# Another order of seven- and eight-product steps, other planned durations, and held-back first loads in a planner-ordered attention trunk

## The chip, the cores and the metric

The kernel runs on one core of one Trainium2 chip. The metric is the time of one execution on the device, in microseconds. Five engines of the core matter here: TensorE (PE in the profile) multiplies matrices, VectorE (DVE) and ScalarE (ACT) work on elements, GpSimd (POOL) and SyncE (SP) issue transfers.

## The reference

One layer of a decoder: RMS norm of x, projection to q, k, v and a gate, attention in which every weight is a product of sigmoids (stick breaking), a SiLU gate, an output projection, the residual, and a last RMS norm. All is float32.

```python
D_MODEL, SEQ, N_HEADS, HEAD_DIM = 4096, 256, 32, 128

def attn_branch(xn, w_in, w_out):              # w_in (4096, 16384), w_out (4096, 4096)
    q, k, v, g = jnp.split(xn @ w_in, 4, axis=-1)
    o = stick_breaking_attention(to_heads(q), to_heads(k), to_heads(v))
    return (o * jax.nn.silu(g)) @ w_out

def one_block(qb, k, v):                        # of 128 queries, for every head
    z = qb @ k.T / sqrt(128)
    log_fail = where(causal, log_sigmoid(-z), 0)
    suffix = reverse_cumsum(log_fail) - log_fail
    a = where(causal, exp(log_sigmoid(z) + suffix), 0)
    return a @ v

h = x + attn_branch(rms_norm(x, norm_attn), w_in, w_out)
return rms_norm(h, final_norm)
```

## The kernel before

**Numbers.** TensorE works on float32 numbers cut in two: a high part (a cast by ScalarE, `wh` for weights) and a low part (the number minus its high part, by VectorE, `wl`). Every product of two blocks is three matmuls of 128x128 by 128x512: high by high, high by low, low by high (`mm3`, L792). The left operands are the stationary forms, `sh` and `sl` for x, `oh` and `ol` for the heads' outputs.

**Units and steps.** The columns of the weights are worked on in 20 units, one after the other: units 0 to 15 are w_in (two heads each: 256 columns of q, k, gate and v), units 16 to 19 are w_out (1024 columns each). A unit has 16 steps, one for each 256 rows of the weights. In a step, two tiles of weights of 512 KB each are loaded (`raw`, by SyncE in two transfers each) and multiplied as a 2x2 matrix of blocks with the 2x2 matrix of the left side. There are three ways to do it. Units 0 and 16 are plain: eight products into four accumulators. In all other units a step has eight products (`EIGHT_PARTS`, L82) or, in the manner of Strassen and Winograd, seven (`SEVEN_PARTS`, L76), into accumulators b1 to b7, each one bank of PSUM, which are combined only once, at the end of a unit. The list `SEVEN` (L43) says which ten of the sixteen steps have seven. In the last unit (19), the steps run in the order `LAST_STEPS` (L50) and those in `EIGHT_LAST` (L52) have eight.

A seven takes one product less, but more of the other engines. Its weights are four parts: one whole tile, half a tile, and two whole tiles of sums and differences. VectorE computes three whole lows (`wl`, 128x1024), a half low (it lies in a tile of the `wh` kind, so the profile calls it wh<-raw,wh) and three sums (raw<-raw,raw twice and raw<-raw, `sums`, L406). A fourth sum is made by GpSimd with a transfer that adds in place (`add_block`, L383). An eight takes two whole lows and no sum. Five places exist for whole lows (`LOWS`), seven for highs and seven for raw tiles.

**The end of a unit.** `combine` (L688) empties the accumulators into two tiles, `qk_sb` and `gv_sb`. Its order on VectorE is: add bank 6 to gv_sb, add bank 7 to gv_sb, scale and add bank 2 to qk_sb, then bank 4 to qk_sb, then bank 5 to both halves of gv_sb, then bank 3. Bank 4 waits for `early`, which is banks 6 and 7 on VectorE and three scalings on ScalarE. A bank can be written by the next unit only when it is empty. The next unit's step 0 is an eight, and takes banks 2, 2, 4, 4, 5, 5, 3, 3.

**Heads.** In the steps after a unit of w_in, the attention of its two heads runs between the products (`head`, L809; `gate`, L775): transposes, scores, a scan and the output on TensorE, some element-wise work on ScalarE and VectorE. The heads' results go to DRAM and come back as the left side of w_out.

**Who sets the order.** All instructions are emitted in an order found by a planner, `Plan` (L105), that simulates five engines while the program is built. Pieces of work ask for an engine with a cost, from `vector_ns`, `scalar_ns` and `tensor_ns` (L93 to L102), and a key; whenever an engine is free, the planner gives it the ready piece with the lowest key (`turn`, L221). A piece that depends on another is ready only when the simulated engine has finished that one; meanwhile the engine takes another that is ready. What comes out is a fixed order for each engine; on the chip the engines then run those orders with semaphores for the dependencies, at the durations that the chip has. Nothing of the planner runs on the chip.

A key is a time at which the result is due, counted in products: `PRODUCT` = 3 x `tensor_ns(512)` (L302) is 680.25 ns, `first[n]` is when part n of the weights is first used, `place_of[u, s]` when step s of unit u begins. Lows have `first[n]`, or 4 us earlier for the first two parts of a seven (L440); casts 2 us earlier still; sums 3 us before their use (L416). The evictions of `combine` have the start of the next unit, `place_of[u + 1, 0]`, plus 0 to 4 ns (L691), on ScalarE 2 us less. `ten` (L335) is the heads' work on TensorE; it has precedence over products.

**The first loads.** `load` (L364) issues the raw tiles in the order of their use, each as soon as one of the seven places for raw tiles is free. In unit 0 the left side is loaded and cut at the same time: `blocks_of` (L535) loads 256 KB of x transposed (`xs`) for each step through the same queue of SyncE, once the step four before has been used, and writes the stationary forms `sh` and `sl` that step needs; at its end it tells ("form", "s", step). Blocks of x for the norm (`xr`) go through that queue too.

Of the kernel before, what the change touches and what calls it, by code (L numbers as in the profile page):

```python
# [28 lines left out]
W = 2 * CW  # L29
# [10 lines left out]

SEVEN = (1,3,4,6,7,9,10,12,13,14)  # L43
RAW_BUFS = 7
HIGHS = 7
LOWS = 5
ROWS = 4
SINGLES = 2

LAST_STEPS = (0, 1, 2, 3, 5, 4, 6, 13, 7, 8, 9, 14, 10, 12, 11, 15)  # L50

EIGHT_LAST = (12, 13, 14)  # L52
KEPT = 5
LAST_ORDER = (5, 4, 2, 3)

# [4 lines left out]
ON_SCALAR = ((1, 3, 5), (1, 3))  # L60
AHEAD, SUMS_AHEAD = 4.0, 3.0
BLOCKS_LATER = 2


PLAIN = {"C11": 1, "C21": 6, "C12": 7, "C22": 3}
# [33 lines left out]


def tensor_ns(n):
    return 0.4167 * n + 13.4 if n > 128 else 109.0  # L102


class Plan:  # L105
# [135 lines left out]
def kernel(  # L241
# [41 lines left out]
    for u, (kind, w, cols) in enumerate(units):  # L283
        for s in (step_at(u, k) for k in range(NS)):
            quads.append(tuple((w, c, s) for c in cols))
            if kind == "plain":
                which = [plain_part(0, PLAIN["C11"], PLAIN["C21"]), plain_part(1, PLAIN["C12"], PLAIN["C22"])]
            else:
                which = SEVEN_PARTS if s in SEVEN and not (u == LAST and s in EIGHT_LAST) else EIGHT_PARTS
            for i, (k, place, prods) in enumerate(which):  # L290
                parts.append(
                    dict(u=u, s=s, i=i, tile=(len(quads) - 1, k), place=place, prods=prods, quad=len(quads) - 1,
                         seven=which is SEVEN_PARTS, size=place.stop - place.start)
                )
# [24 lines left out]
        return nc.here + 1e3 * c  # L319


    def dve(emit, n, key=None, **kw):
        n = n if isinstance(n, tuple) else (n,)
        cost = sum(vector_ns(m) for m in n) + 122 * (len(n) - 1)
        return nc.work("vector", cost, emit, soon() if key is None else key, **kw)

    def act(emit, n, key=None, **kw):
# [5 lines left out]
    FULL_P, FULL_S = (P,) * 2, (W,) * 2  # L333

    def ten(emit, *n):  # L335
        return nc.work("tensor", 90 + sum(tensor_ns(m) for m in n), emit, nc.here - 1e4, wait=400)

    def moved(engine, emit, sizes, key, after=None, hold=False, adds=False, wait=0):
        issue = 550 if engine == "gpsimd" else 330
# [24 lines left out]
    def load():  # L364

        seven = [parts[quad_parts[q][0]]["seven"] for q in range(len(quads))]
        tiles = [(2 * q - 1.5 if t and seven[q] else 2 * q + t, q, t) for q in range(len(quads)) for t in range(2)]
        for _, q, t in sorted(tiles):
            w, blocks, s = quads[q][t]
            yield nc.take("raw")  # L370
            r = raw[q, t] = wp.tile([P, HG, KT, CW], F32, tag="raw", name=f"raw{q}_{t}", bufs=RAW_BUFS)
            if t and seven[q]:
                nc.start(add_block(q))

            def both():
# [30 lines left out]
    def sums(q):  # L406

        a, b, c, d = quad_parts[q]
        one, two = raw[q, 0], raw[q, 1]
        for k in range(2):  # L410
            tile_left[q, k] += 1

        def add(to, at_, f, g, key, op=ALU.add):
            return dve(
                lambda: nc.vector.tensor_tensor(out=to[:, :, at_, :], in0=f, in1=g, op=op), W,
                key - SUMS_AHEAD * 1e3,  # L416
            )

        yield nc.until(("lows", a), ("T3", q))
        yield add(one, 0, one[:, :, 0, :], two[:, :, 0, :], first[c], ALU.subtract)  # L420
        yield nc.until(("lows", b))
        yield add(two, 1, one[:, :, 0, :], two[:, :, 1, :], first[c])
        nc.tell(("sums", c))
        yield add(one, 1, one[:, :, 0, :], one[:, :, 1, :], first[d])
        nc.tell(("sums", d))
        for k in range(2):
            tile_done(q, k)
# [5 lines left out]
    def piece(n, c, there):  # L433

        p = parts[n]
        yield nc.until(*there)
        full = raw[p["tile"]][:, :, p["place"], :][:, :, c, :].rearrange("p i c (h e) -> p c i h e", e=RUN)
        h = wh[n][:, c]
        size = (c.stop - c.start) * W
        key = first[n] - (AHEAD * 1e3 if p["seven"] and p["i"] < 2 else 0)  # L440
        yield act(lambda: nc.scalar.copy(h, full), size, key - 2.0 * 1e3)
        if p["size"] == KT:
            if c.start == 0:
                yield nc.take("wl")
                wl[n] = by_runs(wp.tile([P, KT * W], F32R, tag="wl", name=f"wl{n}", bufs=LOWS))
                nc.tell(("lowslot", n))
            else:
                yield nc.until(("lowslot", n))
        l = wl[n][:, c]
        if n == 0:  # L450
            yield nc.until(("sh", c.start))
        yield dve(lambda: minus(l, full, h), size, key)
        for k in range(c.start, c.stop):
            nc.tell(("low", n, k))
        low_done(n)
# [33 lines left out]
    forms = {}  # L489

    def new_forms(i, what):
        n = len(SEVEN_FORMS if i in SEVEN else EIGHT_FORMS)
        h = sp.tile([P, n, P], F32R, tag=f"xh{i}", name=f"{what}h{i}")
        l = sp.tile([P, n, P], F32R, tag=f"xl{i}", name=f"{what}l{i}")
        forms[i] = h, l
        return h, l
# [18 lines left out]
    def sums_of(i, y, what, key):  # L515

        tt = nc.vector.tensor_tensor
        if i not in SEVEN:
            yield from differences(i, y, key)
        else:  # L520

            def four():
                tt(out=y[:, 0, :], in0=y[:, 1, :], in1=y[:, 0, :], op=ALU.subtract)
                tt(out=y[:, 1, :], in0=y[:, 3, :], in1=y[:, 1, :], op=ALU.subtract)
                tt(out=y[:, 3, :], in0=y[:, 0, :], in1=y[:, 3, :], op=ALU.subtract)
                tt(out=y[:, 2, :], in0=y[:, 2, :], in1=y[:, 3, :], op=ALU.add)

            yield dve(four, (P, P, P, P), key)
            yield from both_parts(i, slice(4, 7), y[:, 1:4, :], key)

# [157 lines left out]
    def combine(u, one, two, what):  # L688

        bank = ev[u]  # L690
        key = place_of[u + 1, 0]  # L691

        row = [rs["v"][:, t : t + 1] if u < OUT0 else 1.0 for t in range(NT)]

# [3 lines left out]
        def add_scaled(to, b, f, n, t):  # L698
            if u >= OUT0:
                return add(to, b, f, n)  # L700
            return dve(
                lambda: nc.vector.scalar_tensor_tensor(
                    out=to, in0=bank[b], scalar=row[t], in1=f, op0=ALU.mult, op1=ALU.add
                ),
                W, key + n,
            )

        def scaled(to, f, t):
# [231 lines left out]
    def blocks_of_heads(s):  # L940
# [9 lines left out]
        yield from both_parts(s, slice(0, 4), y, key)  # L950
        nc.tell(("form", "o", s))
        key = min(place_at(OUT0, s + SUMS_LATER), place_of[OUT0 + 1, s] - 3e3)
        if s in SEVEN and s < NS - 1:
            nc.give("gh")
            yield nc.until(("used", OUT0, s))
            y = yield from heads_of(s, key)
# [358 lines left out]
```

## Time and profile before

| what | value |
|---|---|
| time, median of 3 runs | 1736.43 us (1734.35 to 1738.91) |
| the profiled execution | 1736.38 us, of which the profile's span is 1734.4 us |
| mean granted clock of TensorE | 0.998 of full speed |
| ScalarE, GpSimd: busy share | 70%, 19% |
| first product of unit 0, of unit 1, of unit 16 | 5.9 us, 96.5 us, 1386.2 us |
| last matmul | 1722.5 us |

How to read it: the profile is of one execution. PE, DVE, ACT, POOL and SP are the engines; a busy share is the time in which an engine executes, so what is left is waiting. Nearly all instructions are issued through one helper, so they all carry the line L124, and one goes by the names of the tiles, written out<-in: acc<-wh,sl is a matmul of a weight's high part with a low left side into an accumulator. A wait names whose result ended it. In a timeline, a row has the start, the duration, the engine, the operation and the tiles, and a number in brackets is the time that the engine was idle before it; consecutive instructions of one kind are one row with a count. Engines overlap the end of one instruction with the start of the next, so durations add up to more than the distance of the starts.

### The profile page before, as it was taken

The page shows a single profiled execution, that of the slowest core. Times are in us where ns is not written, and L with a number is a line of the kernel's source. Part 1 is how long each engine was busy: PE and PEld are TensorE (multiplying, and loading weights), DVE is VectorE, ACT ScalarE, POOL GpSimd, SP SyncE. Part 2 cuts the span into 40 slices and gives each one's busy share as a digit, 9 for nine tenths or more (in the row PEclk, how much of TensorE's full clock was granted, in tenths as well). Part 3 has the DMA queues.
Part 4 walks back from the last instruction along what each step waited for, and adds up shares of the span by engine and source line. Part 5 has one row for each costly group of instructions (what it writes and reads, how often), then busy time and mean ns, then how long its engine had stood idle before and what let it go on. Part 6 is the DMA issues. An engine that isn't in the chain of part 4 may idle for free. (4 is left out here: it accounts for less than half of the span.)

```text
span 1734.4 us, 25312 instructions
## 1 busy us (share of the span) xinstructions
PE 1709.5 (99%) x7735; PEld 1413.1 (81%) x7735; DVE 1634.4 (94%) x2106; ACT 1209.9 (70%) x1640; POOL 334.7 (19%) x407
## 2 busy tenths in 40 slices
PE   9999999999999999999999999999999999999997
PEld 7788788888888888888888888888888888888785
DVE  8889999999999999999999999999999987999997
ACT  8976767676767676767676767676767675666654
POOL 0012222222222222222212222222222112112220
PEclk9999999999999999999999999999999999999999
DMA  9968887879787878787879787979787978899895
GB/s 361 313 170 237 224 237 219 242 215 249 206 256 207 256 207 256 209 258 203 262 199 263 200 258 201 258 197 260 198 257 198 284 237 249 244 269 259 229 305 190
DMA packets 249385, 413.82 MB, mean 239 GB/s; under 512 B 28129, under 2 KB 73441, under 8 KB 249249
## 3 DMA queue, kind: packets, MB, share of 16 engines
q1 hardware_dynamic: 194544, 354.24, 61.6%
q0 software_dynamic: 54416, 57.70, 20.4%
q8 instruction: 60, 0.98, 0.2%
q14 instruction: 77, 0.62, 0.1%
q10 hardware_dynamic: 288, 0.28, 0.0%
HBM read 403.98 MB, written 8.13 MB: 238 GB/s over the span
## 5 line engine op out<-in xcount | busy, mean ns | idle before, releaser
L124 ACT CAST wh<-raw 128x1024 fp32r<-128x1024 f32 (+1 forms) x995 | 922.3, 970 | 379.6 <-DVE raw L124 183.0
L124 DVE TENSOR_TENSOR wl<-raw,wh 128x1024 fp32r<-128x1024 f32 (+1 forms) x818 | 974.6, 1217 | 67.5 <-PE acc L124 31.3
L124 PE MATMUL acc<-wh,sh 128*128 128x512 f32 x2048 | 784.8, 395 | 8.1 <-DVE qk_sb L124 7.6
L124 PE MATMUL acc<-wh,sl 128*128 128x512 f32 x1898 | 732.8, 386 | 0.5 <-DVE sl L124 0.5
L124 PE MATMUL acc<-wl,sh 128*128 128x512 f32 x1748 | 675.7, 387 | 1.5 <-DVE wl L124 1.5
L124 POOL DMA_DIRECT2D raw<-in_w_in_dram x300 | 262.2, 982 | 1046.1 <-DMA raw<-in_w_in_dram 423.5
L124 PEld LDWEIGHTS acc<-wh,sh 128*128 128x128 f32 x2048 | 384.6, 188 | 92.4 <-DVE qk_sb L124 13.6
L124 PEld LDWEIGHTS acc<-wh,sl 128*128 128x128 f32 x1898 | 355.8, 187 | 73.8 <-DVE sl L124 1.0
L124 PEld LDWEIGHTS acc<-wl,sh 128*128 128x128 f32 x1748 | 328.3, 188 | 63.9 <-DVE wl L124 4.4
L124 DVE TENSOR_TENSOR raw<-raw,raw 128x512 f32<-128x512 f32 x354 | 242.3, 684 | 6.8 <-DMA raw<-in_w_in_dram 2.8
L124 PE MATMUL acc<-wh,oh 128*128 128x512 f32 x512 | 194.3, 388 | 0.0
L124 PE MATMUL acc<-wh,ol 128*128 128x512 f32 x485 | 187.1, 386 | 0.0
L124 PE MATMUL acc<-wl,oh 128*128 128x512 f32 x458 | 177.3, 387 | 1.9 <-DVE wl L124 1.9
L124 DVE TENSOR_TENSOR wh<-raw,wh 128x512 fp32r<-128x512 f32 x177 | 120.8, 683 | 2.0 <-ACT wh L124 2.0
L124 DVE TENSOR_TENSOR raw<-raw 128x512 f32<-128x512 f32 x177 | 120.8, 682 | 0.0
L124 PEld LDWEIGHTS acc<-wh,oh 128*128 128x128 f32 x512 | 96.0, 188 | 19.1
L124 PEld LDWEIGHTS acc<-wh,ol 128*128 128x128 f32 x485 | 90.9, 187 | 18.6 <-DVE ol L124 0.2
L124 PEld LDWEIGHTS acc<-wl,oh 128*128 128x128 f32 x458 | 85.8, 187 | 21.1 <-DVE wl L124 4.4
L124 POOL DMA_DIRECT2D raw<-in_w_out_dram x54 | 47.0, 964 | 177.4 <-DVE wl L124 64.3
L124 ACT ACTIVATE f<-f 128x384 f32<-128x384 f32 x96 | 50.4, 525 | 3.0
L124 ACT COPY qkT<-tr 128x512 f32<-128x512 f32 x32 | 18.7, 583 | 36.3 <-PE tr L124 36.3
L124 ACT CAST oh<-p 128x512 fp32r<-128x512 f32 (+3 forms) x46 | 21.0, 466 | 19.0 <-DVE p L124 16.0
(83 smaller groups left out, 780.8 us busy)
## 6 DMA issues: line engine op xcount, KB each, us to landing
raw<-in_w_in_dram SPq DMA_DIRECT2D x1024, 256.0 KB, 4.1
raw<-in_w_out_dram SPq DMA_DIRECT2D x256, 256.0 KB, 4.4
raw<-in_w_in_dram POOLq DMA_DIRECT2D x300, 128.0 KB, 4.8
p<-spill POOLq DMA_DIRECT2D x28, 256.0 KB, 4.6
raw<-in_w_out_dram POOLq DMA_DIRECT2D x54, 128.0 KB, 4.9
xr<-in_x_dram SPq DMA_DIRECT2D x16, 256.0 KB, 5.3
xres<-in_x_dram SPq DMA_DIRECT2D x16, 256.0 KB, 5.9
out_dram<-h SPq DMA_DIRECT2D x16, 256.0 KB, 2.8
```

The lines of the kernel that those rows point to most:

```text
L124: return self.tc.keep_in_program_order(getattr(self.engine, name)(*args, **kw))
```

## The change

Five things change. The list of seven-product steps is another, so that steps of seven come two in a row and then one of eight (before, it was one, then pairs, and at the end three in a row); the order of the last unit and its steps of eight are other ones to fit it. A second name, `SEVEN_OUT`, for the list in w_out is introduced, with the same steps. The planner's durations change: a product is 677.25 instead of 680.25 ns, a low costs 10 ns more, a sum of `sums` 10 ns more if it adds and 120 if it subtracts, a scaled eviction of `combine` 60 ns more, the heads' work on TensorE 50 ns less. The keys of `combine` are 1.5 us lower (`SOONER`). And in unit 0, from step 4 on, `load` waits with the raw tiles of a step until the stationary forms of the step three before are written (`FORMS_BEHIND`).

```diff
-SEVEN = (1,3,4,6,7,9,10,12,13,14)
+SEVEN = (1, 2, 4, 5, 7, 8, 10, 11, 13, 14)
+SEVEN_OUT = SEVEN
+SOONER = 1.5
...
-LAST_STEPS = (0, 1, 2, 3, 5, 4, 6, 13, 7, 8, 9, 14, 10, 12, 11, 15)
-
-EIGHT_LAST = (12, 13, 14)
+LAST_STEPS = (0, 1, 3, 2, 4, 6, 5, 13, 7, 9, 8, 14, 10, 11, 12, 15)
+
+EIGHT_LAST = (11, 13, 14)
...
+FORMS_BEHIND = 3
...
 def tensor_ns(n):
-    return 0.4167 * n + 13.4 if n > 128 else 109.0
+    return 0.4167 * n + 12.4 if n > 128 else 109.0
...
-                which = SEVEN_PARTS if s in SEVEN and not (u == LAST and s in EIGHT_LAST) else EIGHT_PARTS
+                which = SEVEN_PARTS if s in (SEVEN if u < OUT0 else SEVEN_OUT) and not (u == LAST and s in EIGHT_LAST) else EIGHT_PARTS
...
-    def dve(emit, n, key=None, **kw):
+    def dve(emit, n, key=None, more=0, **kw):
         n = n if isinstance(n, tuple) else (n,)
-        cost = sum(vector_ns(m) for m in n) + 122 * (len(n) - 1)
+        cost = sum(vector_ns(m) for m in n) + 122 * (len(n) - 1) + more
...
     def ten(emit, *n):
-        return nc.work("tensor", 90 + sum(tensor_ns(m) for m in n), emit, nc.here - 1e4, wait=400)
+        return nc.work("tensor", 40 + sum(tensor_ns(m) for m in n), emit, nc.here - 1e4, wait=400)
...
         for _, q, t in sorted(tiles):
             w, blocks, s = quads[q][t]
+            if FORMS_BEHIND < q < NS:
+                yield nc.until(("form", "s", q - FORMS_BEHIND))
             yield nc.take("raw")
...
         def add(to, at_, f, g, key, op=ALU.add):
             return dve(
                 lambda: nc.vector.tensor_tensor(out=to[:, :, at_, :], in0=f, in1=g, op=op), W,
-                key - SUMS_AHEAD * 1e3,
+                key - SUMS_AHEAD * 1e3, more=120 if op == ALU.subtract else 10,
             )
...
-        yield dve(lambda: minus(l, full, h), size, key)
+        yield dve(lambda: minus(l, full, h), size, key, more=10)
...
-        key = place_of[u + 1, 0]
+        key = place_of[u + 1, 0] - SOONER * 1e3
...
                 lambda: nc.vector.scalar_tensor_tensor(
                     out=to, in0=bank[b], scalar=row[t], in1=f, op0=ALU.mult, op1=ALU.add
                 ),
-                W, key + n,
+                W, key + n, more=60,
             )
```

In `new_forms`, `sums_of` and `blocks_of_heads`, `SEVEN` becomes `SEVEN_OUT` for the left side of w_out; the two lists are equal.

More of the change, by code (lines that the diff above doesn't have):

```diff
@@ L491, in new_forms @@
     def new_forms(i, what):
-        n = len(SEVEN_FORMS if i in SEVEN else EIGHT_FORMS)
+        n = len(SEVEN_FORMS if i in (SEVEN if what == "s" else SEVEN_OUT) else EIGHT_FORMS)
         h = sp.tile([P, n, P], F32R, tag=f"xh{i}", name=f"{what}h{i}")
@@ L517, in sums_of @@
         tt = nc.vector.tensor_tensor
-        if i not in SEVEN:
+        if i not in (SEVEN if what == "n" else SEVEN_OUT):
             yield from differences(i, y, key)
@@ L952, in blocks_of_heads @@
         key = min(place_at(OUT0, s + SUMS_LATER), place_of[OUT0 + 1, s] - 3e3)
-        if s in SEVEN and s < NS - 1:
+        if s in SEVEN_OUT and s < NS - 1:
             nc.give("gh")
```

## The prediction

> **What bounds the kernel now.** The page comes first, for the busy shares and the granted clock.
>
> ```profile
> span 1734.4 us, 25312 instructions
> ...
> PE 1709.5 (99%) x7735; PEld 1413.1 (81%) x7735; DVE 1634.4 (94%) x2106; ACT 1209.9 (70%) x1640; POOL 334.7 (19%) x407
> ...
> PEclk9999999999999999999999999999999999999999
> ```
>
> TensorE (PE) is busy for 99% of the span, at a clock of nine tenths or more in every slice. The change keeps the number of products: ten of sixteen steps have seven products before and after, and in the last unit three of them run as eight in both. So it can only change the time in which TensorE waits. The view of waits, for TensorE, in three stretches of the span (0 to 96 us, the plain first unit; 100 to 1380 us, the other units of w_in; 1380 us to the end, w_out):
>
> ```profile
> PE acc L124 <- DVE wl L124: 0.8, 1, 0.8
> PE acc L124 <- DVE sl L124: 0.5, 1, 0.5
> PE acc L124 <- ACT sh L124: 0.4, 1, 0.4
> ```
> ```profile
> PE acc L124 <- DVE qk_sb L124: 7.6, 14, 1.1
> PE acc L124 <- DVE wl L124: 0.8, 3, 0.4
> ```
> ```profile
> PE acc L124 <- DVE wl L124: 2.0, 5, 0.8
> ```
>
> The columns are the sum in us, the count and the longest. That is 1.7 + 8.4 + 2.0 = 12.1 us in 25 waits. The timeline of TensorE shows what one costs, at the mildest and at the worst of the fourteen:
>
> ```profile
> 784.52 0.39 PE L124 MATMUL acc<-wl,sh 128*128 128x512 f32 x1
> 784.74 0.39 PE L124 MATMUL acc<-wh,sl 128*128 128x512 f32 x1
> 785.36 0.49 PE L124 MATMUL acc<-wh,sh 128*128 128x512 f32 x1 [0.22 <-DVE qk_sb L124]
> ```
> ```profile
> 441.14 0.39 PE L124 MATMUL acc<-wh,sl 128*128 128x512 f32 x1
> 442.62 0.50 PE L124 MATMUL acc<-wh,sh 128*128 128x512 f32 x1 [1.09 <-DVE qk_sb L124]
> ```
>
> Starts lie 0.22 us apart, at the wait 785.36 - 784.74 = 0.62: 0.40 us are lost where the row names 0.22. At 442.62 it is 1.26 for 1.09. So a wait costs its entry and 0.17 us more, the part of a matmul (0.39 long, 0.22 apart) that otherwise runs under the one before it. All 25 cost 12.1 + 25 x 0.17 = 16.4 us, and the fourteen 7.6 + 14 x 0.17 = 10.0. No order of the work can give more than that: 1736.4 (the profiled execution, equal to the median of the runs) - 16.4 = 1720.0.
>
> Now who makes TensorE wait. The windows, for units 5 and 7 of w_in and for the first two mixed units of w_out, 17 and 18 (cut where the timeline shows the first product of a unit):
>
> ```profile
> core 0: us, PE busy (x) PEld busy (x) DVE busy (x) ACT busy (x) POOL busy (x), PEclk, DMA share, GB/s
> 5.90:96.50 90.60, 88.87 (x389) 72.26 (x389) 78.83 (x140) 78.48 (x148) 5.44 (x6) 1.00 0.96 325
> ...
> 440.00:526.50 86.50, 85.41 (x392) 70.90 (x390) 83.08 (x103) 61.46 (x82) 18.06 (x21) 1.00 0.82 232
> 612.30:698.00 85.70, 85.48 (x392) 70.93 (x391) 82.36 (x102) 60.95 (x80) 18.05 (x21) 1.00 0.81 230
> ...
> 1477.90:1558.30 80.40, 79.98 (x355) 66.22 (x354) 80.23 (x100) 52.85 (x67) 16.80 (x20) 1.00 0.87 253
> 1558.30:1640.10 81.80, 80.65 (x356) 66.15 (x355) 80.89 (x97) 51.21 (x65) 17.92 (x23) 1.00 0.91 262
> ```
>
> VectorE (DVE) is idle for 3.3 of 85.7 us in a unit of w_in, and for 0.2 and 0.9 us in units 17 and 18. It is a second bound, just behind TensorE. 79.98 us for 355 matmuls is 0.2253 each, or 0.676 a product. The timeline of VectorE at the same two boundaries:
>
> ```profile
> 772.35 4.62 DVE L124 TENSOR_TENSOR wl<-raw,wh 128x1024 fp32r<-128x1024 f32 x4
> 776.89 0.68 DVE L124 TENSOR_TENSOR wh<-raw,wh 128x512 fp32r<-128x512 f32 x1
> 777.49 1.22 DVE L124 TENSOR_TENSOR wl<-raw,wh 128x1024 fp32r<-128x1024 f32 x1
> 778.63 0.68 DVE L124 TENSOR_TENSOR gv_sb<-acc,gv_sb 128x512 f32<-128x512 f32 x1
> 779.23 1.22 DVE L124 TENSOR_TENSOR wl<-raw,wh 128x1024 fp32r<-128x1024 f32 x1
> ...
> 781.62 0.68 DVE L124 TENSOR_TENSOR raw<-raw,raw 128x512 f32<-128x512 f32 x1
> 782.22 0.68 DVE L124 TENSOR_TENSOR wh<-raw,wh 128x512 fp32r<-128x512 f32 x1
> ...
> 783.43 1.22 DVE L124 TENSOR_TENSOR wl<-raw,wh 128x1024 fp32r<-128x1024 f32 x1
> 784.56 0.74 DVE L124 SCALAR_TENSOR_TENSOR qk_sb<-acc,scalars,qk_sb 128x512 f32<-128x512 f32 x1
> 785.22 0.74 DVE L124 SCALAR_TENSOR_TENSOR gv_sb<-acc,scalars,gv_sb 128x512 f32<-128x512 f32 x1
> ```
> ```profile
> 435.89 0.68 DVE L124 TENSOR_TENSOR gv_sb<-acc,gv_sb 128x512 f32<-128x512 f32 x1
> ...
> 441.82 0.74 DVE L124 SCALAR_TENSOR_TENSOR qk_sb<-acc,scalars,qk_sb 128x512 f32<-128x512 f32 x1
> ```
>
> By `combine`, the first gv_sb row empties bank 6 and the last qk_sb row bank 4, for which TensorE waits in step 0 of the next unit. From the start of the one to the restart of TensorE it is 785.36 - 778.63 = 6.73 us in the mild case and 442.62 - 435.89 = 6.73 in the bad one: a rigid chain. What differs is when VectorE comes to it. TensorE asked at 784.96 and 441.36, which is 6.33 and 5.47 us after the chain's start. Bank 6 had its last product eleven products before the one that waits (one of step 14, eight of step 15, two of step 0): 11 x 0.676 + 0.22 - 0.39 = 7.27 us before TensorE asks. VectorE therefore came 0.9 us late in the mild case and 1.8 us in the bad one, with its backlog of lows and sums; had it come at once, bank 4 would have been free 7.27 - 6.73 = 0.5 us early. The fourteen waits are backlog of VectorE at the end of a unit.
>
> **The change, part by part.** *Order of sevens.* A seven costs VectorE three whole lows at 1.13 (four take 4.62 us, the last 1.22 of it: 3.40 / 3), a half low at 0.60 (776.89 to 777.49) and three sums at 0.60 (781.62 to 782.22): 5.8 us, against 7 x 0.676 = 4.73 on TensorE. It loses 1.07 us. An eight costs two lows, 2.27, against 5.41: it gains 3.1. Before, steps 12, 13 and 14 are sevens and the unit ends with a backlog grown by 3.2 us; after, only 13 and 14 are, behind an eight, and it grows by 2.1. So VectorE comes to bank 6 about 1.07 us sooner. That covers every boundary wait but the last 0.2 us of the longest (1.26): of 10.0 us some 9.4 go. From this I take off 2.4 (0.17 us a unit), because the 6.73 us hold lows put between dependent steps (779.23 and 783.43), and another order may put more there: 7.0 us gained. The ends are 0 and 10.0.
>
> The three waits for wl in w_in lie in that third seven; the first of them, eight us before unit 2 begins (window 181.80):
>
> ```profile
> 173.84 0.49 PE L124 MATMUL acc<-wl,sh 128*128 128x512 f32 x1 [0.40 <-DVE wl L124]
> ```
> ```profile
> 181.80:268.40 86.60, 85.53 (x392) 70.93 (x392) 83.24 (x104) 61.44 (x82) 18.03 (x21) 1.00 0.83 230
> ```
>
> With two sevens in a row VectorE is 1.07 us further along there, and the longest of the three costs 0.40 + 0.17: 0.8 + 3 x 0.17 = 1.3 us gained; ends 0 and 1.3.
>
> By the Trainium skill, "VectorE: DVE Perf Modes", section "The DRAIN you can't avoid", the next operation of VectorE doesn't start until the pipe is empty, so a low would hold it for its whole 1.22 us and a seven would lose about 1.7, not 1.07. Then all 10.0 us would go, and the sum below would be 1723.9. The row of four lows in 4.62 us, not 4.88, speaks against it.
>
> In w_out VectorE is busy for 80.23 of 80.40 us. The number of sevens is the same, so an order only moves the 2.0 + 5 x 0.17 = 2.9 us of waits about: I take 0. The upper end follows from the plan's durations.
>
> *Durations of the plan.* They emit nothing; they change what the planner puts in front of what. A product goes from 680.25 to 677.25 ns, nearer 676. Scaled evictions get 60 ns more, 0.66 us, which is what 784.56 to 785.22 shows. A subtracting sum gets 120 ns more, though the trace has 0.60 where something else follows it: with ten sevens a unit, the plan holds VectorE to be slower by 10 x 0.12, and by 0.7 for the 10 ns on 52 lows and 20 adding sums, 1.9 us a unit. An engine that is faster than planned comes early and waits for others. In w_in its 3.3 us of idle time hide that; in three mixed units of w_out nothing does: up to 3 x 1.9 = 5.7 us lost. I take 0, since the order there follows keys more than times. Products of heads lose 50 ns of planned cost: 0.
>
> *SOONER.* The keys of `combine` fall by 1.5 us, on ScalarE from 2.0 to 3.5 us ahead of the unit. The keys of step 15's lows are 5.4 and 2.7 us ahead and still come first; of step 0's they are 0 and 2.7 behind, and at the boundary the evictions won against these already whenever they were ready. I take 0; the ends are 0 and one low, 1.13 us a unit, inside the 10.0 above. What is put back is lows of the next unit, which have lead.
>
> *Loads held back.* In unit 0, from step 4 on, a step's raw loads are issued only once the stationary forms of three steps before are written. The wait is the planner's; on the chip only SyncE's queue gets another order: the xs and xr loads go ahead, all later raw loads stand behind, and ScalarE's casts, VectorE's lows and GpSimd's adding transfers wait for those. The window of unit 0 has the DMA engines busy for 0.96, and the wait for sl and sh falls in step 7, whose xs load queued behind raw loads:
>
> ```profile
> 46.50 0.50 PE L124 MATMUL acc<-wh,sh 128*128 128x512 f32 x1 [0.44 <-ACT sh L124]
> ...
> 47.75 0.49 PE L124 MATMUL acc<-wh,sl 128*128 128x512 f32 x1 [0.52 <-DVE sl L124]
> ```
> ```profile
> raw<-in_w_in_dram SPq DMA_DIRECT2D x1024, 256.0 KB, 4.1
> ```
>
> These cost 0.9 + 2 x 0.17 = 1.2 us: gained. A held load has some three steps, 3 x 5.4 us, until it is used, and lands in 4.1; if that cover failed, it would cost up to one landing, 4.1 us. The wait for wl at 13 us lies in step 1, which nothing holds back: it stays.
>
> *The last unit's order* keeps nine eights and seven sevens: 0.
>
> Sum: 7.0 + 1.3 + 1.2 = 9.5, so 1736.4 - 9.5 = 1726.9 us.
>
> **The rivals.** *All goes* (0.10): 10.0 + 1.3 + 1.2 = 12.5, 1723.9. *The boundary wait stays* (0.16): the chain of 6.73 us gets one low longer, 1.13, and eats what VectorE gains by coming sooner; 1.3 + 1.2 go, 1733.9. For it: the same gap in every unit. Against it: it varies from 0.40 to 1.26 with an unchanged order. The Trainium skill, "Perfetto Trace Analysis", section "Identifying the Most-Contended Engine", reads consistent bubbles as a possible lack of SBUF or PSUM for the next tile, which no order would cure; by it the time would be this one. *VectorE waits in w_out* (0.06): 1726.9 + 5.7 = 1732.6. *Slower* (0.12): steps 1 and 2 are now both sevens, right behind the evictions, where step 2 was an eight that gave 3.1 us back. If VectorE enters step 1 with less than the 2.1 us that two sevens lose, the second one makes TensorE wait in each of 18 mixed units for about 1.07: + 19.3 - 1.2, 1754.5. For it: the evictions go first. Against it:
>
> ```profile
> 790.88 1.23 DVE L124 TENSOR_TENSOR wl<-raw,wh 128x1024 fp32r<-128x1024 f32 x1 [0.73 <-PE acc L124]
> ```
>
> 5.5 us after TensorE's restart VectorE waits for TensorE to free one of its five places for lows: its lead is full there.
>
> **How the numbers follow.** The forecast has 0.56, with the rivals 1.00. A measurement tells apart about 0.3%, 5.2 us: faster is below 1731.2 (0.56 + 0.10), the same up to 1741.6 (0.16 + 0.06), slower 0.12. The range goes from the floor, 1720.0, to 1740.0, which is nothing gained and 4 us lost to a load or in w_out; outside stay the slower case and a little.
>
> **What would show it.** Right: TensorE's waits for qk_sb fall from 7.6 us to about 2, bank 6 is taken within half a us of its last product, waits for sl and sh are gone, units of w_in take 85.3 to 85.6 us. Wrong: the fourteen waits stay with a chain longer than 6.73; or waits for wl in steps 1 and 2; or more idle time of VectorE in units 17 to 19; or waits for raw loads in the first 96 us.

## The result, and the profile after

| | before | after |
|---|---|---|
| time, median | 1737.07 us (6 runs, 1734.35 to 1738.91) | 1725.36 us (6 runs, 1721.32 to 1728.04) |
| ratio | | 0.9932, 95% interval 0.9915 to 0.9949 |
| profiled execution, its span | 1736.38, 1734.4 us | 1725.08, 1722.3 us |

The change gains 0.7%. The page of after, first lines:

```profile
span 1722.3 us, 25298 instructions
...
PE 1704.4 (99%) x7735; PEld 1415.7 (82%) x7735; DVE 1634.9 (95%) x2106; ACT 1199.3 (70%) x1640; POOL 335.6 (19%) x407
```

TensorE and VectorE have the instructions that they had before, in the same number, and VectorE has the same busy time. What changed is waiting. The waits of TensorE, in the first unit (0 to 96 us), the other units of w_in (100 to 1372 us) and w_out (from 1372 us), in this order:

```profile
PE acc L127 <- ACT wh L127: 0.4, 1, 0.4
```
```profile
PE acc L127 <- DVE qk_sb L127: 0.7, 1, 0.7
```
```profile
PE acc L127 <- DVE wl L127: 3.8, 3, 1.9
PE tr L127 <- DVE gated L127: 0.2, 1, 0.2
```

Of the fourteen waits for qk_sb one is left, and none for wl in w_in. In w_out the waits grew from 2.0 to 4.0 us. The lengths of the stages, cut at the first product of a unit in the timeline (us):

| | to the first product | unit 0 | units 1 to 15 | 16 | 17 | 18 | 19 and tail | span |
|---|---|---|---|---|---|---|---|---|
| before | 5.91 | 90.55 | 1289.72 | 91.68 | 80.44 | 81.75 | 94.36 | 1734.42 |
| after | 6.15 | 89.30 | 1275.73 | 92.10 | 82.78 | 82.47 | 93.77 | 1722.29 |
| difference | +0.24 | -1.25 | -13.99 | +0.42 | +2.34 | +0.72 | -0.59 | -12.1 |

So w_in gains 14.0, unit 0 1.2, and w_out gives 2.9 back. First the boundary of unit 9, now at 774.83 us, in the timeline of VectorE:

```profile
769.17 0.68 DVE L127 TENSOR_TENSOR gv_sb<-acc,gv_sb 128x512 f32<-128x512 f32 x1
769.77 1.22 DVE L127 TENSOR_TENSOR wl<-raw,wh 128x1024 fp32r<-128x1024 f32 x1
...
775.11 0.74 DVE L127 SCALAR_TENSOR_TENSOR qk_sb<-acc,scalars,qk_sb 128x512 f32<-128x512 f32 x1
```

Bank 6 is taken at 769.17, 5.66 us before the unit begins. Its last product ends 5.94 us before, so VectorE comes 0.28 us after it; it came 0.9 to 1.8 us after it before. The chain from there to the end of the row that empties bank 4 is 769.17 to 775.85 = 6.68 us. It had that length before: 778.63 to 785.30, the end of the row at 784.56, is 6.67 (the forecast's 6.73 runs on to the restart of TensorE). Then TensorE, after and before, from the unit's first product to the head's scores (z):

```profile
774.83 0.38 PE L127 MATMUL acc<-wh,sh 128*128 128x512 f32 x1
...
776.18 0.39 PE L127 MATMUL acc<-wh,sh 128*128 128x512 f32 x1
776.41 0.38 PE L127 MATMUL acc<-wl,sh 128*128 128x512 f32 x1
...
779.37 0.82 PE L127 MATMUL z<-qkT 128*128 128x128 f32 x4
```
```profile
783.62 0.38 PE L124 MATMUL acc<-wh,sh 128*128 128x512 f32 x1
...
785.69 0.39 PE L124 MATMUL acc<-wl,sh 128*128 128x512 f32 x1
...
787.02 0.39 PE L124 MATMUL acc<-wh,sl 128*128 128x512 f32 x1
787.37 0.47 PE L124 MATMUL acc<-wh,sh 128*128 128x512 f32 x1
...
788.82 0.82 PE L124 MATMUL z<-qkT 128*128 128x128 f32 x4
```

After, this stretch takes 779.37 - 774.83 = 4.54 us; before, 788.82 - 783.62 = 5.20: 0.66 us more, though the only named wait there is 0.22 and the forecast made it 0.40. The rest stands in rows without a bracket. The matmul behind the delayed one starts 785.69 - 785.36 = 0.33 us after it, not 0.23; and at 787.37 the first product into the next bank starts 0.35 after the one before, a wait of 0.12 that the view doesn't name. At the worst boundary of before (440.02) the stretch is 6.05 us: 1.51 lost, where the forecast had 1.26. So each boundary cost about 0.25 us more than the forecast made of the named wait. Over the fourteen boundaries the stretch loses 13.5 us before, against 4.54 us each, and 1.5 after.

The window of this unit of after, of units 17 and 18 of after, and of unit 9 of before:

```profile
774.83:859.84 85.01, 85.01 (x392) 70.99 (x390) 82.67 (x102) 60.15 (x80) 18.33 (x22) 1.00 0.83 233
...
1463.30:1546.10 82.80, 80.88 (x356) 66.13 (x355) 80.97 (x101) 52.09 (x67) 15.81 (x19) 1.00 0.87 247
1546.10:1628.50 82.40, 80.50 (x355) 66.06 (x354) 80.57 (x97) 51.43 (x67) 17.84 (x22) 1.00 0.90 256
```
```profile
783.62:869.29 85.67, 85.45 (x391) 70.91 (x390) 82.33 (x102) 60.98 (x80) 18.06 (x21) 1.00 0.82 231
```

The unit is 85.67 - 85.01 = 0.66 us shorter, which is the boundary's 0.66 and nothing else. In unit 17 TensorE is now idle for 1.9 us (82.80 - 80.88), in one wait, in the second seven of steps 10 and 11; the other two waits for wl in w_out are in unit 18, also in the second seven of a pair (0.56 us in step 5, 1.32 in step 11). VectorE, which was idle for 0.2 us in unit 17, is idle for 1.8:

```profile
1523.18 0.49 PE L127 MATMUL acc<-wl,oh 128*128 128x512 f32 x1 [1.91 <-DVE wl L127]
```
```profile
1483.90 0.69 DVE L127 TENSOR_TENSOR raw<-raw,raw 128x512 f32<-128x512 f32 x1 [0.77 <-DMA raw<-in_w_out_dram]
...
1510.80 0.69 DVE L127 TENSOR_TENSOR h<-h,xres 128x512 f32<-128x512 f32 x1 [0.68 <-DMA xres<-in_x_dram]
...
1520.77 3.49 DVE L127 TENSOR_TENSOR wl<-raw,wh 128x1024 fp32r<-128x1024 f32 x3
```

It loses 0.77 to a late raw load and 0.68 to a late load of x, and when TensorE comes to step 11 its lows are not done: the three lows at 1520.77 run one behind the other, and TensorE goes on at 1523.18. That the two late loads are the cause is not shown.

### The profile page after: what moved, and what is told of

Same layout as the page of the kernel before. It is cut to its first block, busy times and chain, and to the rows that moved or that the text cites. A ratio compares the mean times of both kernels' runs of the same rounds, so it can differ in the third digit from the quotient of the medians.

```text
span 1722.3 us, 25298 instructions
## 1 busy us (share of the span) xinstructions
PE 1704.4 (99%) x7735; PEld 1415.7 (82%) x7735; DVE 1634.9 (95%) x2106; ACT 1199.3 (70%) x1640; POOL 335.6 (19%) x407
## 5 line engine op out<-in xcount | busy, mean ns | idle before, releaser
L127 DVE TENSOR_TENSOR wl<-raw,wh 128x1024 fp32r<-128x1024 f32 (+1 forms) x818 | 974.9, 1218 | 33.7 <-PE acc L127 13.5
L127 PEld LDWEIGHTS acc<-wh,ol 128*128 128x128 f32 x485 | 90.9, 187 | 18.4
L127 POOL DMA_DIRECT2D p<-spill x28 | 17.0, 682 | 85.3 <-ACT gl L127 26.8
```

Of the source, the lines that this page charges most:

```text
L127: return self.tc.keep_in_program_order(getattr(self.engine, name)(*args, **kw))
```

## The experiments

All ratios are to the kernel before, on the same chip.

### Order, durations, and all but the durations

**e1_order_only** is the kernel before with the new lists:

```diff
-SEVEN = (1,3,4,6,7,9,10,12,13,14)
+SEVEN = (1, 2, 4, 5, 7, 8, 10, 11, 13, 14)
...
-LAST_STEPS = (0, 1, 2, 3, 5, 4, 6, 13, 7, 8, 9, 14, 10, 12, 11, 15)
+LAST_STEPS = (0, 1, 3, 2, 4, 6, 5, 13, 7, 9, 8, 14, 10, 11, 12, 15)
...
-EIGHT_LAST = (12, 13, 14)
+EIGHT_LAST = (11, 13, 14)
```

**e2_durations_only** is the changed kernel with the old three lists and these two values, so that only the durations are new:

```diff
-SOONER = 1.5
+SOONER = 0.0
...
-FORMS_BEHIND = 3
+FORMS_BEHIND = 99
```

**e3_no_durations** is the changed kernel with the old durations: these two lines, and no `more` of lows, sums and scaled evictions.

```diff
-    return 0.4167 * n + 12.4 if n > 128 else 109.0
+    return 0.4167 * n + 13.4 if n > 128 else 109.0
...
-        return nc.work("tensor", 40 + sum(tensor_ns(m) for m in n), emit, nc.here - 1e4, wait=400)
+        return nc.work("tensor", 90 + sum(tensor_ns(m) for m in n), emit, nc.here - 1e4, wait=400)
```

> The kernel before with the new lists of steps alone (SEVEN, LAST_STEPS, EIGHT_LAST); the plan's durations, the keys of combine and the first loads stay. Theory of the order (the boundary waits are backlog of VectorE from three sevens in a row): TensorE's waits for qk_sb fall from 7.6 us to under 2, units 1 to 15 take 1276 to 1280 us instead of 1289.7, and the time is 1722 to 1728. Rival of the durations (VectorE is planned too fast, so evictions stand too late in its order): the waits stay above 5 us, units 1 to 15 above 1285, the time 1732 or more. Unit 0 keeps its 90.6 us in both.

> The changed kernel with the old lists of steps, no SOONER and no held loads: the plan's new durations alone. Theory of the order: three sevens in a row still delay VectorE, waits for qk_sb stay at 5 us or more and the waits for wl at step 14 stay; 1732 to 1738. Rival of the durations: the waits for qk_sb fall under 2 us and units 1 to 15 take under 1280; 1722 to 1728.

> The changed kernel with the old durations of the plan (order, SOONER and held loads stay). For units 1 to 15 the theory of the order expects 1276 to 1279 us as in the changed kernel; the rival of the durations 1283 or more. For w_out: if the new durations make VectorE come early and wait, units 17 and 18 fall from 165.3 us to about 162 and the time to about 1722; if the loss there comes from the order of the steps, they stay at 165 and the time at 1725.

| | time | ratio | units 1 to 15 | units 17 + 18 |
|---|---|---|---|---|
| e1_order_only | 1733.59 us | 0.9979 (0.9969 to 0.9989) | 1280.54 | 168.05 |
| e2_durations_only | 1734.90 us | 0.9991 (0.9981 to 1.0001) | 1287.21 | 162.12 |
| e3_no_durations | 1732.41 us | 0.9975 (0.9965 to 0.9985) | 1280.76 | 169.64 |
| before, after | | | 1289.72, 1275.73 | 162.19, 165.25 |

The waits of TensorE in units 1 to 15 of e2, and the window of a unit of e1, in which no wait for qk_sb is left:

```profile
PE acc L127 <- DVE qk_sb L127: 7.8, 13, 1.0
```
```profile
607.90:693.21 85.31, 85.31 (x391) 70.90 (x390) 82.40 (x102) 60.13 (x80) 18.05 (x21) 1.00 0.80 231
```

The order takes the boundary waits away, the durations don't. But the times of e1 and e3 miss the ranges that were expected: the order alone gains only 9.2 us in w_in and loses 5.9 in units 17 and 18. With the new durations on top the units of w_in fall from 85.3 to 85.0 us, 5 us in all, and units 17 and 18 lose 3 instead of 5.9 to 7.5.

The 5 us in w_in stand mostly in one place that the view of waits leaves out, the second head's scores (z), here in e1:

```profile
630.45 0.39 PE L124 MATMUL acc<-wh,sl 128*128 128x512 f32 x1
630.83 0.92 PE L124 MATMUL z<-qkT 128*128 128x128 f32 x4
631.40 0.57 PE L124 MATMUL acc<-wh,sh 128*128 128x512 f32 x1
```

From the matmul ahead of the scores to the product behind them it is 631.40 - 630.45 = 0.95 us, where the changed kernel has 0.69. In units 2 to 15 this loses 4.6 us in e1 and 4.5 in e3, and nothing in the changed kernel.

Here is what w_out loses without the durations, in e1 and e3: one long wait at the beginning of unit 18.

```profile
1555.74 0.79 PE L124 MATMUL acc<-wh,oh 128*128 128x512 f32 x1 [3.48 <-DVE h L124]
```
```profile
1553.74 0.49 PE L127 MATMUL acc<-wh,oh 128*128 128x512 f32 x1 [4.01 <-DVE h L127]
```

VectorE's evictions of unit 17 (h) stand behind sums and lows of the next unit in its fixed order, and in e1 two of these wait themselves, 0.99 us for a raw load and 0.63 for a cast. So the durations, for which the forecast took 0 and feared 5.7 us of loss, bring some 7 us on top of the new order (e3 has 0.9975 of the time before, the whole change 0.9932); with the old order they bring nothing clear of noise (e2).

### Which durations

**e6_pe_durations_old** is the changed kernel with the two edits of TensorE's planned durations that e3 shows, and VectorE's new ones. **e7_dve_durations_old** is the opposite: VectorE's three go back.

```diff
-                key - SUMS_AHEAD * 1e3, more=120 if op == ALU.subtract else 10,
+                key - SUMS_AHEAD * 1e3,
...
-        yield dve(lambda: minus(l, full, h), size, key, more=10)
+        yield dve(lambda: minus(l, full, h), size, key)
...
-                W, key + n, more=60,
+                W, key + n,
```

> The changed kernel with the old planned durations of TensorE alone (a product 680.25 ns, heads' work 50 ns more). Units took 85.3 us each without any of the new durations and 85.0 with all; the 0.3 us are waits of the heads' scan matmuls. Theory of TensorE (planned too slow, so its order has the scan too early): units 1 to 15 take 1280 us. Rival (VectorE planned too fast): they stay at 1276. For w_out the theory of VectorE's durations expects units 16 to 18 at 257.4 us as in the changed kernel; the theory of TensorE's 261 or more.

> The changed kernel with the old planned durations of VectorE alone (no 120, 60 and 10 ns). Mirror of the run with TensorE's old durations: by the theory of VectorE units 1 to 15 take 1280 us and units 16 to 18 take 261 us or more, with a wait of TensorE for h of some 3.5 us at the start of unit 18; by the theory of TensorE 1276 and 257.4.

e6: 1723.34 us, 0.9923 (0.9908 to 0.9938), units of w_in at 85.02 (1274.83 for units 1 to 15), units 16 to 18 at 258.5, no wait for h. e7: 1728.27 us, 0.9954 (0.9939 to 0.9969), units 1 to 15 at 1278.67, units 16 to 18 at 261.7, a wait of 3.2 us for h at the beginning of unit 18, and in w_in:

```profile
PE acc L127 <- DVE qk_sb L127: 2.1, 5, 0.7
```

VectorE's durations carry what w_out gains: without them the wait for h is there, with them alone it is not. In w_in it is either set: the scores of the second head lose nothing in e6 nor in e7, and eight units of e7 take 84.97 to 85.03 us. What e7 loses in w_in is boundary waits, in the other six units (five have an entry in the view).

### The third seven

**e5_third_seven** is the changed kernel with the eight of step 12 at step 11, so that a unit ends with three sevens as it did before.

```diff
-SEVEN = (1, 2, 4, 5, 7, 8, 10, 11, 13, 14)
+SEVEN = (1, 2, 4, 5, 7, 8, 10, 12, 13, 14)
...
-EIGHT_LAST = (11, 13, 14)
+EIGHT_LAST = (12, 13, 14)
```

> The changed kernel with one seven moved from step 11 to step 12, so that a unit again ends with three sevens (12, 13, 14) ahead of the last eight; all else is as changed. Theory of the third seven: VectorE has 1.07 us more backlog at the boundary; waits for qk_sb come back in most of the 14 units (4 us or more in all) and units 1 to 15 take 1281 to 1290 us instead of 1275.7. Rival (any order that begins with two sevens gives the gain, or the durations now cover a third): waits for qk_sb stay under 1.5 us and the units under 1279.

1725.63 us, 0.9934 (0.9919 to 0.9949), and no wait for qk_sb in the view, as the rival has it; but the units of w_in take 85.33 us and units 1 to 15 1279.29, between the two ranges (units 17 and 18 take 163.09 instead of 165.25, which hides that in the time). The view leaves out short waits. TensorE at the boundary of 862.23, from the unit's first product to the head's scores:

```profile
862.23 0.38 PE L127 MATMUL acc<-wh,sh 128*128 128x512 f32 x1
...
863.35 0.39 PE L127 MATMUL acc<-wh,sl 128*128 128x512 f32 x1
863.74 0.49 PE L127 MATMUL acc<-wh,sh 128*128 128x512 f32 x1
...
865.41 0.39 PE L127 MATMUL acc<-wh,sl 128*128 128x512 f32 x1
865.75 0.46 PE L127 MATMUL acc<-wh,sh 128*128 128x512 f32 x1
...
867.18 0.82 PE L127 MATMUL z<-qkT 128*128 128x128 f32 x4
```

The first products into the next two banks start 0.39 and 0.34 us after the matmul ahead of them, where the changed kernel has 0.23 both times. The stretch takes 867.18 - 862.23 = 4.95 us against 4.54 and it does so at all fourteen boundaries (4.95 to 4.96): 0.41 us lost at each, none of it in the view, where a mild boundary of before loses 0.66. So moving this one seven brings the boundary loss back in good part. The rows of VectorE ahead of the same boundary, with its last stop and the eviction of bank 6:

```profile
846.04 1.23 DVE L127 TENSOR_TENSOR wl<-raw,wh 128x1024 fp32r<-128x1024 f32 x1 [0.21 <-PE acc L127]
...
857.01 0.68 DVE L127 TENSOR_TENSOR gv_sb<-acc,gv_sb 128x512 f32<-128x512 f32 x1
```

Bank 6 is taken 862.23 - 857.01 = 5.22 us before the next unit, where the changed kernel has 5.66: a third seven makes VectorE 0.44 us later there, not 1.07. In the changed kernel VectorE uses part of what it saves to stand still: 0.53 us at 848.38 (the row stands in the next section), where e5 has no named stop any more.

### The first eight

What makes the rest of the loss before? VectorE gains on TensorE until its lead is full; then it stands still, and its backlog can only grow from there. Before, it stood still 7 us into a unit, so the eight of step 2 that follows might give nothing back. **e9_first_eight_later** moves it, in the kernel before.

```diff
-SEVEN = (1,3,4,6,7,9,10,12,13,14)
+SEVEN = (1,2,4,6,7,9,10,12,13,14)
...
-LAST_STEPS = (0, 1, 2, 3, 5, 4, 6, 13, 7, 8, 9, 14, 10, 12, 11, 15)
+LAST_STEPS = (0, 1, 3, 2, 5, 4, 6, 13, 7, 8, 9, 14, 10, 12, 11, 15)
```

> The kernel before, with one step moved: the first eight of a mixed unit comes at step 3 instead of step 2 (sevens at 1, 2, 4, 6, 7, 9, 10, 12, 13, 14; the unit still ends with three sevens, and the planned durations are the old ones). Theory (VectorE's backlog grows from the last point at which it stood full of lows; an eight at step 2 comes while it is full and gives back nothing, so one eight is wasted): with the eight at 3 it is used, VectorE reaches bank 6 some 2 us earlier, the waits of TensorE for qk_sb fall from 7.6 us in 14 to at most 2 us, units 1 to 15 take 1279 to 1283 us (1289.7 before), the time is 1727 to 1732 us. Rival (what counts is the order of the later steps, which is as before from step 5 on): 14 waits of 7 to 8 us stay, units 1 to 15 at 1288 to 1291, 1735 to 1738 us.

1739.30 us, 1.0016 (1.0007 to 1.0025), units 1 to 15 at 1285.89: both expectations missed. The time is longer although w_in is shorter, since unit 0 takes 92.20 us and unit 17 83.07. The waits of TensorE in units 1 to 15, and the row of VectorE that takes bank 6 ahead of the boundary of 868.41:

```profile
PE acc L124 <- DVE qk_sb L124: 3.7, 14, 0.6
```
```profile
863.41 0.68 DVE L124 TENSOR_TENSOR gv_sb<-acc,gv_sb 128x512 f32<-128x512 f32 x1
```

Fourteen waits stay, of half the sum: VectorE takes bank 6 at 868.41 - 863.41 = 5.00 us before the boundary, in nearly each unit, which is what the better units of before have (4.99 at 783.62), without the worse ones (4.13 at 440.02). So the wasted early eight falls. What is the same in e9 and in before is the last stop of VectorE, 18.4 us before the boundary. This stop in before (the unit ends at 869.29), and the last that the view names in after (859.84):

```profile
850.93 2.36 DVE L124 TENSOR_TENSOR wl<-raw,wh 128x1024 fp32r<-128x1024 f32 x2 [0.64 <-ACT wh L124]
```
```profile
848.38 1.23 DVE L127 TENSOR_TENSOR wl<-raw,wh 128x1024 fp32r<-128x1024 f32 x1 [0.53 <-PE acc L127]
```

| | last named stop, us before the boundary | bank 6 taken, us after its last product | first product to scores, us | lost at the 14 boundaries, us |
|---|---|---|---|---|
| before (better units; the last column all) | 18.4 | 0.95 | 5.20 | 13.5 |
| e9 | 18.4 | 0.94 | 5.20 | 9.8 |
| e5 | 16.2 | 0.72 | 4.96 | 5.8 |
| e1 | 6.7, the one before it 13.6 | 0.34 | 4.58 | 1.7 |
| after | 11.5 | 0.28 | 4.54 | 1.5 |

The first columns are of the commonest kind of unit, and the last sums what the stretch takes over 4.54 us. The later in a unit VectorE last stood still, the sooner it is at bank 6 and the less the boundary costs, down to the last two rows, which are alike. Only e5 and after differ in one seven alone; the other rows are cases that agree, not a proof. In one boundary of e2 (524.63) the last stop is 16.2 us before it, bank 6 comes at 0.72 and the stretch takes 4.98 us: the figures of e5, which has the same durations and the same three sevens at the end, but another beginning. At the other thirteen boundaries of e2 VectorE is later, because a cast just ahead of bank 6 comes late, in twelve of them behind a raw load (ScalarE of e2, boundary at 868):

```profile
861.19 1.05 ACT L127 CAST wh<-raw 128x1024 fp32r<-128x1024 f32 x1 [1.88 <-DMA raw<-in_w_in_dram]
```

Late loads are a second part. After, VectorE waits nine times for raw loads in w_in; behind seven of these the next boundary is as early as elsewhere, and behind the two longest, of 2.43 and 1.99 us, come the units of 85.40 and 86.01 us, the second with the one wait that is left. There a cast inside the boundary's chain waits for a raw load and the chain takes 7.71 us instead of 6.68 (the row of the view of waits for VectorE, then a row of ScalarE and one of TensorE):

```profile
DVE raw L127 <- DMA raw<-in_w_in_dram: 9.7, 9, 2.4
```
```profile
1110.10 1.05 ACT L127 CAST wh<-raw 128x1024 fp32r<-128x1024 f32 x1 [1.97 <-DMA raw<-in_w_in_dram]
```
```profile
1117.32 0.50 PE L127 MATMUL acc<-wh,sh 128*128 128x512 f32 x1 [0.65 <-DVE qk_sb L127]
```

### The loads held back, and SOONER

**e8_loads_not_held** and **e10_sooner_zero** are the changed kernel with one value each:

```diff
-FORMS_BEHIND = 3
+FORMS_BEHIND = 99
```
```diff
-SOONER = 1.5
+SOONER = 0.0
```

> The changed kernel without the held-back first loads. If holding them is what freed the xs loads, the waits for sl and sh come back and unit 0 takes 90.4 to 90.7 us instead of 89.3, 1.2 us in all (the time 1726 to 1727 where the changed kernel has 1725.4). Rival: the new durations or the order did it, and unit 0 stays at 89.0 to 89.4.

> The changed kernel with SOONER at 0: the orders that come out differ in 4 places on VectorE and 4 on ScalarE, and in none on the other engines. Theory: nothing, 1725.4 us, within 2 us; units 1 to 15 at 1275 to 1276.5 us. Rival (the 0.3 us a unit that the full change gains in w_in beyond the order alone comes from earlier keys of the evictions): units 1 to 15 at 1280 us, 1730 us.

e8: 1725.34 us, 0.9936 (0.9919 to 0.9952), the time of the changed kernel and not the 1 us more that was expected; unit 0 takes 90.16 us, between the two ranges, and the waits for sl and sh don't come back. Its profiled execution had a granted clock of 0.90 from 3 to 20 us (1.00 in the others), so TensorE asked later, and this trace can't decide. The windows from 20 to 95 us of e1 and e3, which differ in the held loads and SOONER, do:

```profile
20.00:95.00 75.00, 73.92 (x327) 60.72 (x326) 63.13 (x113) 64.18 (x125) 5.44 (x6) 1.00 0.94 315
```
```profile
20.00:95.00 75.00, 75.00 (x337) 62.38 (x336) 65.05 (x116) 65.26 (x128) 5.44 (x6) 1.00 0.95 321
```

TensorE is busy for 1.08 us more. In the nine profiles with held loads unit 0 takes 88.75 to 89.34 us, in the five without 90.16 to 92.20; from 20 us on none of the nine has a wait of TensorE, and four of the five have one or two of 0.4 to 1.1 us for sl or sh (all but e8). That it shortens the whole time is not shown. e10: 1723.94 us, 0.9931 (0.9918 to 0.9945), units 1 to 15 at 1274.01: SOONER is worth nothing that can be measured (against 0.9932).

### The old pattern in w_out

**e4_out_pattern** is the changed kernel in which units 17 and 18 do their steps in an order that gives the old pattern of sevens and eights; **e11_out_pattern_again** is the same once more, **e12_out_pattern_pe_old** has the durations of e6 too.

```diff
+OUT_STEPS = (0, 1, 3, 2, 4, 6, 5, 7, 9, 8, 10, 12, 11, 13, 14, 15)
...
-step_at = lambda u, k: LAST_STEPS[k] if u == LAST else k
+step_at = lambda u, k: LAST_STEPS[k] if u == LAST else OUT_STEPS[k] if u > OUT0 else k
```

> The changed kernel, with the steps of units 17 and 18 run in an order that puts sevens and eights as before the change (three sevens ahead of the last eight); the set of sevens is the new one. If the loss in w_out comes from the order of the steps, units 17 and 18 fall from 165.3 us to about 162.2 and the time to about 1722; if from the durations or from transfers that land late, they stay at 164 or more. Units 1 to 15 stay at 1276 in both.

> The changed kernel with units 17 and 18 in the old pattern of sevens and eights, once more, on one chip with the changed kernel that has SOONER at 0. Theory (the new order costs 2 to 3 us in unit 17): 1721 us, 3 to 5 us below that one; unit 17 at 80 us. Rival (the first look was chance): no difference, 1724 to 1726 us, unit 17 at 82 to 83 us.

> The changed kernel with the old pattern of steps in units 17 and 18, and with TensorE's planned durations of before (a product 680.25 ns, the heads' work 50 ns more); VectorE's are the new ones. The kernel that had only the second of these took 1723.3 us, 2 us less than the changed kernel in another call. Theory (TensorE's planned durations do not matter in w_in): units 1 to 15 at 1274.5 to 1276 us, and the time within 2 us of the kernel with the old pattern alone, 1719 to 1723 us. Rival (they are needed in w_out, whose margins are small): unit 17 or 18 takes 2 us more, 1723 to 1726 us.

e4: 1721.24 us, 0.9910 (0.9895 to 0.9924). e11: 1720.02 us, 0.9904 (0.9890 to 0.9917). e12: 1719.51 us, 0.9904 (0.9890 to 0.9917). On one chip with e10 (1723.94), which differs in SOONER too, the pattern is worth 3.9 us. Units 17 and 18 take 163.21, 161.58 and 162.17 us (166.44 in e10), and units 1 to 15 of e12 1273.79. Unit 17 of e11 and of e10:

```profile
1461.10:1541.10 80.00, 80.00 (x356) 66.26 (x355) 77.85 (x95) 50.76 (x65) 15.52 (x19) 1.00 0.88 251
```
```profile
1460.70:1545.10 84.40, 82.38 (x356) 67.24 (x355) 80.83 (x100) 52.09 (x66) 16.72 (x20) 0.98 0.86 247
```

With the old pattern TensorE never waits in unit 17, and VectorE has 95 instructions there instead of 100: some of its work fell into unit 16, where it has 16 to 18 us of idle time in these two. (Some 1.6 us of e10's difference is its clock, 0.98 here; after has 82.80 us at 1.00.) VectorE's idle time doesn't tell the two patterns apart: it is 2.15 us in unit 17 of e11. Across all kernels unit 17 takes 80.0 to 80.4 us with the old pattern and 82.2 to 86.2 with the new one, e5's or e9's. The best version is therefore e11 or e12, which can't be told apart, 1.0% under the kernel before.

## Why the prediction was right, and where it was not

**The bound and the mechanism: right.** The waits for qk_sb went but for one, bank 6 is taken at 0.28 us (within half a us was forecast), the chain stayed at 6.7 us, waits for sl and sh are gone, and those for wl in w_in. The order takes the boundary waits away and the durations alone don't (e1 against e2).

**Boundary waits, 7.0 us: mis-sized.** Taking off the 1.3 for wl, w_in gained 12.7. The 2.4 us taken off for a chain that another order would lengthen were not owed: 6.67 became 6.68, but for one late load. And a boundary cost 0.66 where 0.40 was reckoned, 14 x 0.26 = 3.6 us: the entry in the view plus 0.17 holds for the wait itself, but not for the second matmul behind it nor for the unnamed wait at the next bank. All gone would be 10.0 + 3.6 = 13.6; the two units with late loads give back 0.4 + 1.0. For the same reason 1720.0 was not the floor it was called: e12 ran in 1719.5, with waits left.

**"VectorE comes to bank 6 about 1.07 us sooner", by the third seven: mis-sized.** From before to after it comes 0.7 us sooner in the mild units and 1.5 in the worst. With the new durations the third seven alone makes 0.44 us of that, and 0.41 us of TensorE's time at each boundary (e5 against after). The 1.07 us are right as the difference of durations, but they reach the boundary only as far as VectorE doesn't stand still behind that step. In the worst units of before the last stop itself comes 0.9 us later (17.5 us before the boundary), with the same 13.4 us from it to bank 6; why is open, and so is what removed them in e9.

**Lows in the third seven, 1.3: the sum right, the cause not shown.** No wait for wl is left in w_in, but there is none in e2, e5 and e9 either, which keep the third seven.

**Durations, 0: failed.** "The order there follows keys more than times" was wrong: with the old durations the change gains 0.25%, with the new ones 0.68%. In w_in they take 4.5 us of late scores away; in w_out they keep evictions ahead of lows. The rival "VectorE waits in w_out" had their sign reversed.

**w_out's order, 0: failed.** "An order only moves the waits about": it costs 3.9 us with the new durations (e10 against e11) and 5.9 without (units 17 and 18 of e1). The sign that the prediction named, more idle time of VectorE in units 17 to 19, came true, 0.2 to 1.8 us in unit 17, but e11 has it too and no wait of TensorE there. The slower rival, a second seven that makes TensorE wait, came true in w_out: all three waits for wl there, 3.8 us, fall in the second seven of a pair. It did not in w_in, where VectorE's lead is full, as the row quoted against it said.

**Held loads, 1.2: right in the first unit,** where the windows from 20 to 95 us give 1.08 between e1 and e3, and the unit became 1.25 shorter. The wait for wl at 13 us, which was to stay, went too. **SOONER, 0: right** (e10).

So the total of 1726.9 came within 1.5 us of 1725.36 partly by luck, by errors of opposite sign: w_in 5.7 us better than forecast, w_out 2.9 worse. By the Trainium skill, "Perfetto Trace Analysis", section "Optimization Strategy" (the prediction names the section ahead of it), consistent bubbles can mean a lack of SBUF or PSUM for the next tile; the trace disagrees here, for they went with the same banks and tiles. The prediction read the Trainium skill, "VectorE: DVE Perf Modes", section "The DRAIN you can't avoid", too narrowly: the section goes on that an operation that isn't held starts earlier. The four lows in 4.62 us agree with that.

## What to carry to other kernels

A constant wait at a boundary need not mean that a buffer is missing: look back to where the late engine last stood still with a full lead, and see what of its surplus work lies behind that point. An order that helps one stage must be judged in each stage by itself, for one with no slack (w_out) can lose what another gains. And a planner's durations are part of the order: put them near the trace before the order is tuned, and price a wait by the distance of the same two instructions in an undisturbed unit, not by the entry in the view of waits: e5 has no entry and loses 0.41 us at every boundary.

## What the runs showed of the hardware

A wait of TensorE costs more than the idle time named with it: at the mildest boundary 0.66 us for an entry of 0.22, since the following matmul also starts 0.10 us late and a second wait of 0.12 isn't listed. In e5 delays at the same places cost 0.41 us without any entry.

After the three longest waits of TensorE (3.48, 4.01 and 3.2 us, in e1, e3 and e7, all at the beginning of unit 18) the granted clock of that unit was 0.98, 0.96 and 0.97. The whole of it is a few us behind the wait, as the first of these windows of e3 shows beside the whole unit:

```profile
1555.00:1561.00 6.00, 5.38 (x14) 3.85 (x13) 3.68 (x6) 1.04 (x1) 1.76 (x2) 0.50 0.76 239
```
```profile
1553.74:1638.35 84.61, 83.24 (x354) 68.28 (x355) 79.88 (x96) 50.59 (x65) 16.24 (x20) 0.96 0.83 240
```

TensorE is busy in the unit for 83.24 us with the work that takes 80.5 in the changed kernel, 2.7 us more, so the clock behind a long wait can cost two thirds of it again. A shorter wait was followed by it once: in e10 TensorE waits 1.90 us until 1520.60, and from 1521 on the clock is about half:

```profile
1521.00:1524.40 3.40, 3.40 (x10) 2.69 (x9) 3.40 (x5) 1.23 (x2) 0.00 (x0) 0.53 0.97 227
```

After waits of 1.91 us in unit 17 of the changed kernel and of e8, of 1.90 in e6 and of 2.38 in e9, the clock stayed at 1.00. What decides between these cases was not tested.
